# One 128x128 product per direction for the correction of both heads in a chunked delta-rule scan

## The chip, the cores and the metric

The kernel runs as one program on one core of a Trainium2 chip. The metric is the device time of one execution in microseconds. Before the change it is 1182.2 us, the median of three runs (1181.57 to 1183.22 us).

## The reference

Two layers of an encoder over 256 tokens of width 2048. Each layer normalises its input, multiplies it by one wide input matrix, feeds two groups of heads, gates both, and multiplies the result by an output matrix that is added to the residual. One group is windowed attention with a sink per head; the other is the RWKV-7 delta rule, one scan over the tokens per direction, and this is the part that the change touches:

```python
def step(S, inp):
    r_t, w_t, k_t, v_t, kk_t, a_t = inp
    s_kk = jnp.einsum('bhvk,bhk->bhv', S, kk_t)
    S = (S * w_t[:, :, None, :]
         - s_kk[..., None] * (a_t * kk_t)[:, :, None, :]
         + v_t[..., None] * k_t[:, :, None, :])
    return S, jnp.einsum('bhvk,bhk->bhv', S, r_t)
...
for d, rev in enumerate((False, True)):
    ...
    y = y + wkv_scan(rh, heads(decay), kd, vh, kk, heads(a), rev)
```

There are 16 such heads of 64 channels, two directions and 256 steps. The attention masks scores outside a band of 128 tokens on either side.

## The kernel before

**The large matrix products.** The input and output matrices are streamed from HBM as tiles of 128x1024 f32, each split on the chip into a high part (ScalarE, line 241) and the rest (VectorE, line 243). Every 128 contraction rows then cost three matmuls with 256 moving columns (lines 311 to 313): high by high, high by the rest of the activations, rest by high. The queue of these steps is called S; S.run(n) issues n of them.

**The scans** work on pairs of heads, eight pairs p per layer: head 0 of a pair lies in partitions 0 to 63, head 1 in 64 to 127. The 256 tokens are cut into NC = 4 chunks of 64. For each chunk and direction the delta rule becomes a triangular system. scan_p prepares keys, decays and values of a pair. scan_i builds the triangular matrices and inverts all 16 of a pair by doubling levels in f16, with a last refinement; its result, an inverse of 64x64 per head, direction and chunk, is copied out of PSUM into VF (line 966). scan_b then goes through the chunks i = 0 to 3, both directions side by side (direction 1 takes the chunks in reverse), and each chunk has three segments:

- a: right-hand sides (matmuls, line 993), copied to RH (ScalarE, line 995), and the outputs of the chunk before (line 978);
- b: the part of the output that comes from the state (line 1005); the **correction**, the inverse times RH, one 64x64 product per direction and head (line 1011); a product with the identity that carries the state along (line 1014); and two copies of the result into SUV (ScalarE, line 1016), which overwrite the state that lines 1005 and 1014 read;
- c: the new state (matmuls, line 1021, and VectorE, line 1023).

All operands of the correction are f32. Head 0 uses rows and columns 0 to 63 of the array, head 1 rows and columns 64 to 127.

**The order of the work.** TensorE's order is the order of the program text; the order on the other engines is made by a planner from modelled times and priorities, apart from the calls through PA and PV, which keep their order. A layer is a row of windows w. A window has 11 slots; in each slot every generator that is due issues its next segment, in the order of the list in scans(), and then S issues its share of the 64 steps, 17 or 18 matmuls. I call the matmuls of the segments of one slot a burst. A pair p runs scan_p in windows p and p+1, scan_i in p+2 and in slots 0 to 4 of p+3, and scan_b from slot 5 of window p+3 on. The correction of chunk 0 falls in slot 6 and that of chunk 1 in slot 9 of window p+3, those of chunks 2 and 3 in slots 1 and 4 of window p+4. In slots 6 and 9 scan_b of that pair comes after scan_i of the next one; in slots 1 and 4 it comes first.

**What else meets there.** In slot 8 scan_p issues a sum over heads into a PSUM tile pk, which VectorE reads with a reciprocal (kd). In slot 9 scan_p issues another such sum, pbn (both line 706), and scan_i takes a PSUM tile pd (line 937). pk, pbn, pd and scan_i's other tiles (pq and pn among them) come from one pool of two buffers, and pd gets the buffer of pk. In slot 7 the matmuls of line 937 read QF and tt, which ScalarE copies out of the pq of slot 6 (lines 931 and 899).

**The band.** A mask of 128x512 comes from HBM in one piece of 128x960 f32 with other constants (line 353), is cast to bf16 once (line 371), and is used by all attention scores of both layers (line 1092). Attention starts in slot 3 of window 10 of a layer.

Of the kernel before, what the change touches and what calls it, by code (L numbers as in the profile page):

```python
# [9 lines left out]
F32 = mybir.dt.float32  # L10
F32R = mybir.dt.float32r
F16 = mybir.dt.float16
BF16 = mybir.dt.bfloat16
U8 = mybir.dt.uint8
I32 = mybir.dt.int32
AF = mybir.ActivationFunctionType
# [5 lines left out]
T = 256  # L22
# [3 lines left out]
NP = 8  # L26
# [4 lines left out]
NC = T // CHUNK  # L31
# [13 lines left out]

STAGE_P = (([8], [4, 5, 7, 8, 10]), ([9], [0, 1, 3, 4, 5, 6, 7, 8, 9]))
STAGE_I = (list(range(SLOTS)), [0, 1, 2, 3, 4])
STAGE_B = (list(range(5, SLOTS)), [i for i in range(SLOTS) if i != 7], [7])
ATT = [
    [3, 9],  # L50
    [1, 3, 5, 6, 8, 10],
# [82 lines left out]
def hybrid_trunk_kernel(ctx, tc, xT, wi, wv, wo, par, fing, dup, iup, sink, pos, cst, out):  # L134
# [24 lines left out]
    def st(tag, shape, dt=F32, bufs=1):  # L159
        return sp.tile([128, *shape], dt, tag=tag, name=tag, bufs=bufs)  # L160
# [45 lines left out]
    class Norm:  # L206


        def add(self, sums):

            self.ps = wpair("pr")
            pr = self.ps[:, :, 0:1]
            self.rt = rt = st("rt", [2])
            self.dg = st("dg", [2, 128])
            for i, a in enumerate(sums):
                for b in range(2):
                    PE.matmul(pr[:, b], a[:, b * 128 : (b + 1) * 128], ones[:, 0:1], start=(i == 0), stop=(i == len(sums) - 1))
            with tc.high_priority(offset=100):
                V.tensor_scalar(rt, pr[:, :, 0], 1.0 / D, NORM_EPS, op0=ALU.mult, op1=ALU.add)
                G.tensor_tensor(rt, rt, mhalf[:, 0:2], op=ALU.pow)  # L220
                for b in range(2):
                    V.tensor_scalar(self.dg[:, b, :], ident, rt[:, b : b + 1], None, op0=ALU.mult)
# [113 lines left out]
    LV = cp.tile([128, NL, 2, 128], U8, name="LV")  # L336
    AB0, AB1, AL, QF = (cp.tile([128, 2, NC, 64], F16, name=n) for n in ("AB0", "AB1", "AL", "QF"))
    MSK = cp.tile([128, NC, 64], F16, name="MSK")
    EYE, NEYE, EYE2 = (cp.tile([128, 64], F16, name=n) for n in ("EYE", "NEYE", "EYE2"))
    band = cp.tile([128, 512], BF16, name="band")  # L340
    BONES = cp.tile([128, 128], F32R, name="BONES")
    FG = cp.tile([128, NKT], F32, name="FG")
    SK = cp.tile([128, DEPTH * 16], F32, name="SK")
# [3 lines left out]
    def setup():  # L347
        posi = st("t1", [T], I32, bufs=3)
        SY.dma_start(out=posi, in_=pos.to_broadcast([128, T]))
        SY.dma_start(out=FG, in_=fing)  # L350
        SY.dma_start(out=SK, in_=sink.to_broadcast([128, DEPTH * 16]))
        cin = st("mv", [C_N - C_KEEP], bufs=3)
        SY.dma_start(out=cin, in_=cst[:, C_KEEP:C_N])
        for l in range(DEPTH):
            s = DP[:, l, 0:NSH]
            V.tensor_tensor(s, PR[:, l, P_MU0 : P_MU0 + NSH], PR[:, l, P_MU1 : P_MU1 + NSH], op=ALU.add)
            V.tensor_scalar(s, s, -1.0, 1.0, op0=ALU.mult, op1=ALU.add)
            h = DP[:, l, NSH : NSH + 8]
            V.tensor_scalar(h, PR[:, l, P_KA : P_KA + 8], 0.5, None, op0=ALU.mult)
            V.tensor_scalar(DP[:, l, NSH + 8 : NSH + 16], h, -1.0, 1.0, op0=ALU.mult, op1=ALU.add)  # L360
            V.tensor_scalar(DP[:, l, NSH + 16 : NSH + 32], PR[:, l, P_A0 : P_A0 + 16], 0.5, None, op0=ALU.mult)
        V.tensor_scalar(SK, SK, 8.0, None, op0=ALU.mult)
        yield

        V.tensor_copy(
            LV.rearrange("p l s (n x) -> p (l s) n x", x=32),
            cin[:, 512 : 512 + 64 * NL].rearrange("p (n x) -> p n x", x=32).unsqueeze(2).to_broadcast([128, 2 * NL, NC, 32]),
        )
        V.memset(MSK, 1.0)
        V.memset(MSK[:, :, 0:1], 0.0)  # L370
        V.tensor_copy(band, cin[:, 0:512])
        A.activation(BONES, ones, AF.Copy, scale=0.0)
        for r in half:
            A.activation(BONES[r, r], ones[r, r], AF.Copy)
        V.tensor_copy(EYE, cin[:, 512 + 64 * NL : 576 + 64 * NL])
        V.tensor_scalar(NEYE, EYE, -1.0, None, op0=ALU.mult)
        V.tensor_scalar(EYE2, EYE, 2.0, None, op0=ALU.mult)
        yield

        AN = st("VA", [2, T])  # L380
        ang, nn = AN[:, 0], AN[:, 1]
        V.tensor_copy(ang, posi)
        yield
        PV.tensor_scalar(ang, ang, C[:, C_OFF["inv"] : C_OFF["inv"] + 1], None, op0=ALU.mult)
        yield

        def reduce_by(dst, src, period, bits, shift):
            PV.tensor_scalar(nn, src, 1.0 / period, shift, op0=ALU.mult, op1=ALU.add)
            yield
            PV.tensor_scalar(nn, nn, MAGIC, MAGIC, op0=ALU.add, op1=ALU.subtract)  # L390
            yield
            cur = src
            for p in split_const(period, bits, 4):
                PV.scalar_tensor_tensor(dst, nn, -p, cur, op0=ALU.mult, op1=ALU.add)
                cur = dst
                yield

        two_pi = 2.0 * np.pi
        yield from reduce_by(ang, ang, two_pi * 4096.0, 7, 0.0)
        for dst, shift, add in ((SIN, 0.0, 0.0), (COS, 0.25, np.pi / 2)):  # L400
            yield from reduce_by(dst, ang, two_pi, 11, shift)
            if add:
                PV.tensor_scalar(dst, dst, float(add), None, op0=ALU.add)
            PV.tensor_scalar(dst, dst, PI_IN, -PI_IN, op0=ALU.min, op1=ALU.max)
            yield
        for dst in (SIN, COS):
            PA.activation(dst, dst, AF.Sin)
        yield
        PV.tensor_scalar(SIN, SIN, C[:, C_OFF["sgn"] : C_OFF["sgn"] + 1], None, op0=ALU.mult)
        yield  # L410
# [263 lines left out]
    def layer(l):  # L674
# [141 lines left out]
        def scan_i(p, t):  # L816
# [145 lines left out]
                    )  # L962
            for d, c, h in dch:
                PE.matmul(pn[half[h], d, cs(c)], hx(FN, d, c, h), hx(TT, d, c, h), start=False, stop=True, skip_group_check=True)
            VF = st("vf", [2, NC * 64])
            A.activation(VF, pn[:, :, 0:T], AF.Copy)
            t["VF"] = VF
            yield

        def scan_b(p, t):  # L970
# [12 lines left out]
            for i in range(NC):  # L983
# [15 lines left out]
                if i > 0:  # L999
                    outputs(i - 1)  # L1000
                yield
                if i > 0:
                    for d in range(2):
                        for h in range(2):
                            PE.matmul(  # L1005
                                py[half[h], ci[d], :], MV[half[h], d, ci[d], 1, :], SUV[half[h], d, ci[d], h, :],
                                start=False, stop=False, skip_group_check=True,
                            )
                for d in range(2):
                    for h in range(2):  # L1010
                        PE.matmul(pc[half[h], 1, d, :], t["VF"][half[h], d, cs(ci[d])], RH[half[h], d, :], start=True, stop=True)  # L1011
                if 0 < i < NC - 1:
                    for h in range(2):
                        PE.matmul(pS[half[h]], ident[half[h], half[h]], here(h), start=True, stop=False, skip_group_check=True)  # L1014
# [40 lines left out]
        def scans(w):  # L1055

            gens = []
            prep = [(1, STAGE_P[1]), (0, STAGE_P[0])]
            stages = [(lag, scan_p, at[0]) for lag, at in prep]
            stages += [(4, scan_b, STAGE_B[1]), (3, scan_i, STAGE_I[1]), (2, scan_i, STAGE_I[0])]  # L1060
            stages += [(4, scan_b, STAGE_B[2]), (3, scan_b, STAGE_B[0])]
            stages += [(lag, scan_p, at[1]) for lag, at in prep]
            for lag, scan, at in stages:
                p = w - lag
                if 0 <= p < NP:
                    if (scan, p) not in chains:
                        chains[scan, p] = scan(p, L.ts[p])
                    gens.append((chains[scan, p], at))
            return gens

        def scores(j):
# [13 lines left out]
            for h in range(2):  # L1085
# [4 lines left out]
                A.activation(Sc[:, h, :, 256:257], sk.unsqueeze(1).to_broadcast([128, 2, 1]), AF.Copy)  # L1090
                for q in range(2):
                    V.tensor_tensor_reduce(
                        out=Sc[:, h, q, 0:256], in0=ps[:, q * 256 : (q + 1) * 256], in1=band[:, q * 256 : (q + 1) * 256],
                        scale=1.0, scalar=-3e38, op0=ALU.add, op1=ALU.max, accum_out=mx[:, q : q + 1],
                    )
                V.tensor_scalar(mx, mx, sk, -0.125, op0=ALU.max, op1=ALU.mult)
# [29 lines left out]

        def attend():

            scores(0)
            yield  # L1130
            flip(0)
            scores(1)
            yield
            for x in (MH, ML):
                x.more()
            for j in range(8):
                values(j)
                if j < 6:
                    scores(j + 2)
                yield  # L1140
                if j < 7:
                    flip(j + 1)
                    yield

        for w in range(NP + 2):
            window(64, *scans(w), *([(setup_, ROT.get(w, [2, 5, 9, 9]))] if l == 0 else []))
        att = attend()
        window(64, *scans(NP + 2), (att, ATT[0]))
        window(64, *scans(NP + 3), (att, ATT[1]))
        window(64, (att, ATT[2]))  # L1150
# [3 lines left out]

    queue_inputs(0)
    V.memset(QF, 0.0)

    idle = wbank("warm")
    zeros = QF.rearrange("p d c j -> p (d c j)")
# [122 lines left out]
```

## Time and profile before

| | |
|---|---|
| median of three runs | 1182.2 us |
| the profiled execution: its own time | 1180.42 us |
| its span, first to last instruction | 1178.6 us |
| mean granted TensorE clock | 0.994 of full speed |
| TensorE matmul busy | 1149.2 us (98%) |
| VectorE busy | 906.1 us (77%) |
| ScalarE busy | 777.5 us (66%) |
| GpSimd busy | 21.7 us (2%) |
| DMA queue of the loads | 164.21 MB, 42.7% of 16 engines |

PE is TensorE's matmuls, PEld its weight loads, DVE VectorE, ACT ScalarE, POOL GpSimd, SP the engine that issues the DMAs. A row of the timeline gives start, duration, engine, line, operation, the tiles written and read, and the count of instructions merged into it; in brackets stands the idle time before it and what ended it. A form such as 64*64 64x32 is the shape of the weights and of the moving operand. An f32 matmul is recorded as two passes, each with its weight load; those of lines 311 to 313 take one. Matmuls are pipelined: a row's duration contains the way through the array, so the cost of a stream is read from the distances between starts. A recorded idle time begins at the modelled end of the matmul before, so it is shorter than the delay of the start.

### The profile page before, as it was taken

The numbers are of one execution on the slowest core, as the hardware profiler recorded it, in microseconds if no ns is written. First come the engines' busy times: TensorE is split into PE (matmuls) and PEld (weight loads), VectorE is DVE, ScalarE is ACT, GpSimd is POOL, SyncE is SP. The second block draws the span as 40 slices with busy tenths as digits, with TensorE's granted clock in tenths as the row PEclk, the third lists the DMA queues.
The fourth block names the chain that finished last, engine by engine and source line by source line (L and its number), as shares of the span: only waits on it lengthen the run. The fifth ranks groups of instructions, "written<-read, shape, count | busy, mean of one in ns | idle before, by whom it ended". The sixth has DMA issues, their size and how long they took to land. (4 is left out here: it accounts for less than half of the span.)

```text
span 1178.6 us, 38072 instructions
## 1 busy us (share of the span) xinstructions
PE 1149.2 (98%) x16151; PEld 1076.2 (91%) x16151; DVE 906.1 (77%) x2017; ACT 777.5 (66%) x1955; POOL 21.7 (2%) x23
## 2 busy tenths in 40 slices
PE   8999999999999999999999999999999999999996
PEld 6998999989899999899999989999999999899996
DVE  7889978888877677766678988888887767786654
ACT  6666776786775666655556667776786666675552
POOL 0000000000000000000000000000000000000000
PEclk9999999999999999999999999999999999999998
DMA  7544433233333333477654433333333343346653
GB/s 259 167 153 131 130 107 123 96 111 102 107 102 130 130 125 122 138 239 237 212 183 169 136 130 116 115 111 116 97 112 110 119 132 126 108 140 194 212 192 119
DMA packets 60410, 166.63 MB, mean 141 GB/s; under 512 B 7728, under 2 KB 22736, under 8 KB 60240
## 3 DMA queue, kind: packets, MB, share of 16 engines
q1 hardware_dynamic: 60240, 164.21, 42.7%
q8 instruction: 126, 2.06, 0.7%
q14 instruction: 44, 0.36, 0.1%
HBM read 157.37 MB, written 4.19 MB: 137 GB/s over the span
## 5 line engine op out<-in xcount | busy, mean ns | idle before, releaser
L243 DVE TENSOR_TENSOR lo<-raw,hi 128x512 fp32r<-128x512 f32 x560 | 371.8, 687 | 114.9 <-ACT hi L241 109.7
L241 ACT ACTIVATE hi<-raw 128x512 fp32r<-128x512 f32 x560 | 330.0, 625 | 184.8 <-PE pm L312 103.6
L311 PE MATMUL pm<-XHa,hi 128*128 128x256 f32 x832 | 246.3, 296 | 2.6 <-ACT XHa L203 1.2
L311 PE MATMUL pm<-XHb,hi 128*128 128x256 f32 x832 | 243.9, 293 | 0.6 <-ACT XHb L203 0.4
L313 PE MATMUL pm<-XHb,lo 128*128 128x256 f32 x832 | 234.3, 282 | 1.7 <-DVE lo L243 1.7
L312 PE MATMUL pm<-XLb,hi 128*128 128x256 f32 x832 | 234.3, 282 | 0.4 <-DVE XLb L204 0.4
L312 PE MATMUL pm<-XLa,hi 128*128 128x256 f32 x832 | 233.8, 281 | 0.5 <-DVE XLa L204 0.3
L313 PE MATMUL pm<-XHa,lo 128*128 128x256 f32 x832 | 233.2, 280 | 0.4 <-DVE lo L243 0.4
L311 PEld LDWEIGHTS pm<-XHa,hi 128*128 128x128 f32 x832 | 156.4, 188 | 15.1 <-issue 3.2
L311 PEld LDWEIGHTS pm<-XHb,hi 128*128 128x128 f32 x832 | 157.3, 189 | 6.7 <-ACT XHb L203 0.6
L313 PEld LDWEIGHTS pm<-XHb,lo 128*128 128x128 f32 x832 | 157.4, 189 | 2.2 <-DVE lo L243 2.1
L312 PEld LDWEIGHTS pm<-XLb,hi 128*128 128x128 f32 x832 | 157.5, 189 | 0.6 <-DVE XLb L204 0.6
L312 PEld LDWEIGHTS pm<-XLa,hi 128*128 128x128 f32 x832 | 156.8, 188 | 1.0 <-DVE XLa L204 0.9
L313 PEld LDWEIGHTS pm<-XHa,lo 128*128 128x128 f32 x832 | 156.6, 188 | 0.9 <-DVE lo L243 0.9
L1016 ACT ACTIVATE suv<-pcc 64x128 f32<-64x128 f32 x128 | 34.7, 271 | 73.4 <-PE pcc L1014 49.7
L311 PE MATMUL pm<-MHa,hi 128*128 128x256 f32 x256 | 71.9, 281 | 0.0
L313 PE MATMUL pm<-MHa,lo 128*128 128x256 f32 x256 | 71.7, 280 | 0.0
L311 PE MATMUL pm<-MHb,hi 128*128 128x256 f32 x256 | 71.6, 280 | 0.0
L312 PE MATMUL pm<-MLb,hi 128*128 128x256 f32 x256 | 71.6, 280 | 0.0
L312 PE MATMUL pm<-MLa,hi 128*128 128x256 f32 x256 | 71.6, 280 | 0.0
L313 PE MATMUL pm<-MHb,lo 128*128 128x256 f32 x256 | 71.6, 280 | 0.0
L311 PEld LDWEIGHTS pm<-MHa,hi 128*128 128x128 f32 x256 | 48.1, 188 | 0.8 <-issue 0.8
(291 smaller groups left out, 2312.1 us busy)
## 6 DMA issues: line engine op xcount, KB each, us to landing
raw<-wi SPq DMA_DIRECT2D x207, 512.0 KB
raw<-wo SPq DMA_DIRECT2D x64, 512.0 KB
raw<-wv SPq DMA_DIRECT2D x8, 512.0 KB
rrot<-u SPq DMA_DIRECT2D x80, 32.0 KB
vg<-xT SPq DMA_DIRECT2D x16, 128.0 KB
xd<-vg SPq DMA_DIRECT2D x16, 128.0 KB
vg<-xd SPq DMA_DIRECT2D x16, 128.0 KB
g<-dup SPq DMA_DIRECT2D x16, 97.0 KB
```

The source lines that it names most:

```text
L241: A.activation(hi[:, q], raw[:, q], AF.Copy)
L243: V.tensor_tensor(lo[:, q], raw[:, q], hi[:, q].bitcast(F32), op=ALU.subtract)
L311: PE.matmul(pm, wh, rh[:, kk, :], start=(kk == 0), stop=False)
L312: PE.matmul(pm, wh, rl[:, kk, :], start=False, stop=False)
L313: PE.matmul(pm, wl, rh[:, kk, :], start=False, stop=(kk == 15))
L1016: A.activation(here(h), pc[half[h], 1], AF.Copy)
```

## The change

Four things are done together.

- VF becomes a tile of its own for the whole run, [128, 2, NC, 128] f32, filled with zeros by GpSimd at the start. The inverse of head 0 is written to rows 0 to 63 and columns 0 to 63 of each 128x128 block, that of head 1 to rows and columns 64 to 127: two ScalarE copies of 64 partitions in the place of one copy of 128 partitions.
- The correction is one product per direction with 128x128 weights and 64 moving columns, and it stands first in its segment, ahead of line 1005.
- In slots 6 and 9 the segment of scan_b is issued before that of scan_i (a fourth list in STAGE_B).
- The band mask leaves the load at the start (448 instead of 960 columns). Each layer loads it at the beginning of window 9 into a tile under the tag th, and casts it to bf16 under the tag sl just ahead of the first scores. The tile dg of the norm moves to the tag ysq.

```diff
-STAGE_B = (list(range(5, SLOTS)), [i for i in range(SLOTS) if i != 7], [7])
+STAGE_B = ([5, 7, 8, 10], [i for i in range(SLOTS) if i != 7], [7], [6, 9])
...
-            self.dg = st("dg", [2, 128])
+            self.dg = st("ysq", [2, 128])
...
+    VF = cp.tile([128, 2, NC, 128], F32, name="VF")
...
-    band = cp.tile([128, 512], BF16, name="band")
...
-        cin = st("mv", [C_N - C_KEEP], bufs=3)
-        SY.dma_start(out=cin, in_=cst[:, C_KEEP:C_N])
+        cin = st("mv", [C_N - C_KEEP - 512], bufs=3)
+        SY.dma_start(out=cin, in_=cst[:, C_KEEP + 512 : C_N])
...
-        V.tensor_copy(band, cin[:, 0:512])
...
-            VF = st("vf", [2, NC * 64])
-            A.activation(VF, pn[:, :, 0:T], AF.Copy)
-            t["VF"] = VF
+            for h in range(2):
+                A.activation(VF[half[h], :, :, h * 64 : (h + 1) * 64], pn[half[h], :, 0:T].rearrange("p d (c j) -> p d c j", j=64), AF.Copy)
...
+                for d in range(2):
+                    PE.matmul(pc[:, 1, d, :], VF[:, d, ci[d], :], RH[:, d, :], start=True, stop=True)
                 if i > 0:
                     for d in range(2):
                         for h in range(2):
...
-                for d in range(2):
-                    for h in range(2):
-                        PE.matmul(pc[half[h], 1, d, :], t["VF"][half[h], d, cs(ci[d])], RH[half[h], d, :], start=True, stop=True)
...
-            stages += [(4, scan_b, STAGE_B[1]), (3, scan_i, STAGE_I[1]), (2, scan_i, STAGE_I[0])]
+            stages += [(4, scan_b, STAGE_B[1]), (3, scan_b, STAGE_B[3]), (3, scan_i, STAGE_I[1]), (2, scan_i, STAGE_I[0])]
             stages += [(4, scan_b, STAGE_B[2]), (3, scan_b, STAGE_B[0])]
...
+            wide = st("th", [512])
+            SY.dma_start(out=wide, in_=cst[:, C_KEEP : C_KEEP + 512])
+            yield
+            L.band = st("sl", [512], BF16)
+            V.tensor_copy(L.band, wide)
             scores(0)
...
+        att = attend()
         for w in range(NP + 2):
+            if w == NP + 1:
+                next(att)
...
+    G.memset(VF, 0.0)
```

More of the change, by code (lines that the diff above doesn't have):

```diff
@@ L366, in setup @@
             LV.rearrange("p l s (n x) -> p (l s) n x", x=32),
-            cin[:, 512 : 512 + 64 * NL].rearrange("p (n x) -> p n x", x=32).unsqueeze(2).to_broadcast([128, 2 * NL, NC, 32]),
+            cin[:, 0 : 64 * NL].rearrange("p (n x) -> p n x", x=32).unsqueeze(2).to_broadcast([128, 2 * NL, NC, 32]),
         )
@@ L374, in setup @@
             A.activation(BONES[r, r], ones[r, r], AF.Copy)
-        V.tensor_copy(EYE, cin[:, 512 + 64 * NL : 576 + 64 * NL])
+        V.tensor_copy(EYE, cin[:, 64 * NL : 64 + 64 * NL])
         V.tensor_scalar(NEYE, EYE, -1.0, None, op0=ALU.mult)
@@ L1092, in scores @@
                     V.tensor_tensor_reduce(
-                        out=Sc[:, h, q, 0:256], in0=ps[:, q * 256 : (q + 1) * 256], in1=band[:, q * 256 : (q + 1) * 256],
+                        out=Sc[:, h, q, 0:256], in0=ps[:, q * 256 : (q + 1) * 256], in1=L.band[:, q * 256 : (q + 1) * 256],
                         scale=1.0, scalar=-3e38, op0=ALU.add, op1=ALU.max, accum_out=mx[:, q : q + 1],
@@ L1143, in attend @@
                     yield
+        att = attend()
         for w in range(NP + 2):
+            if w == NP + 1:
+                next(att)
             window(64, *scans(w), *([(setup_, ROT.get(w, [2, 5, 9, 9]))] if l == 0 else []))
-        att = attend()
         window(64, *scans(NP + 2), (att, ATT[0]))
```

## The prediction

> **What bounds the kernel now.** I read the page first, then TensorE's waits, then the timelines of slots 4 to 9 of a window in the middle of layer 1.
>
> ```profile
> span 1178.6 us, 38072 instructions
> ## 1 busy us (share of the span) xinstructions
> PE 1149.2 (98%) x16151; PEld 1076.2 (91%) x16151; DVE 906.1 (77%) x2017; ACT 777.5 (66%) x1955; POOL 21.7 (2%) x23
> ```
>
> ```profile
> PE pd L937 <- DVE kd L256: 5.8, 10, 0.7
> ```
>
> ```profile
> PE pd L937 <- ACT tt L899: 2.0, 1, 2.0
> ```
>
> TensorE is busy for 98% of the span. So each part of the change is worth what it adds to TensorE's stream or takes from the few waits in it. The largest of these (total, times, longest, in us) is the wait of pd for the reciprocal kd. ScalarE at 66% looks free; below it turns out not to be so in one place.
>
> **The product itself.** Its present cost and that of its neighbours, from TensorE's timeline:
>
> ```profile
> L1011 PE MATMUL pcc<-rh,vf 64*64 64x64 f32 x512 | 26.1, 220 | 0.0
> ```
>
> ```profile
> 799.33 0.40 PE L706 MATMUL pbn<-ip,BONES 128*128 128x256 f32 x2
> 800.27 0.30 PE L937 MATMUL pd<-QF,tt 64*64 64x32 f16 x16 [0.54 <-DVE kd L256]
> 800.40 0.44 PE L1005 MATMUL py<-suv,mv 64*64 64x64 f32 x8
> 800.66 0.41 PE L1011 MATMUL pcc<-rh,vf 64*64 64x64 f32 x8
> 800.89 0.40 PE L1014 MATMUL pcc<-suv,C 64*64 64x128 f32 x4
> 801.23 0.38 PE L311 MATMUL pm<-XHa,hi 128*128 128x256 f32 x1
> ```
>
> There are 512 records, 8 in each of 64 bursts. From the first start of L1011 to that of L1014 it is 0.23 us: the two heads run at the same time, in separate quarters of the array, so the eight make four steps of 0.058 us. Merging the heads therefore halves a count of instructions that were already running in pairs.
>
> The new form is not in the trace: four records per burst, two per direction, with 128x128 f32 weights and 64 columns. The nearest rows are the sums of the norm, with the same weights and type and one column:
>
> ```profile
> 24.59 0.28 PE L313 MATMUL pm<-XHa,lo 128*128 128x256 f32 x1
> 24.70 1.84 PE L217 MATMUL pr<-C,mv 128*128 128x1 f32 x16
> 26.41 0.37 PE L311 MATMUL pm<-XHa,hi 128*128 128x256 f32 x1
> ```
>
> ```profile
> 250.10 0.45 PE L978 MATMUL py<-suv,GE 128*64 128x64 f32 x8
> 250.48 0.31 PE L937 MATMUL pd<-QF,tt 64*64 64x32 f16 x16
> ```
>
> ```profile
> 412.18 0.28 PE L313 MATMUL pm<-XHa,lo 128*128 128x256 f32 x1
> 412.39 0.45 PE L1011 MATMUL pcc<-rh,vf 64*64 64x64 f32 x8
> 412.77 0.39 PE L311 MATMUL pm<-XHa,hi 128*128 128x256 f32 x1
> ```
>
> Sixteen of them take 26.41 - 24.70 = 1.71 us, 0.107 each, although they stream one column: the weights set the pace. The array is entered without a break (24.59 to 24.70, 0.11), while a change to quarters costs 0.21 (412.18 to 412.39). After a short f32 product the next shape comes 0.15 later: the last of L978 starts at 250.10 + 0.45 - 0.22 = 250.33, L937 at 250.48. So the new product ahead of a burst adds 0.11 to enter, three steps of 0.107 and 0.15 to leave, less the 0.21 that entering the quarters costs today: 0.37 us. The bounds of the step are 0.058 (the present one, if the loads hid) and 0.107; I take the upper one, which the same weights show.
>
> The Trainium skill says the same of the loads in "TensorE: Matmul & The Clock Gate", section "LDWEIGHTS (loading the stationary operand)", as columns over 1.2, 107 ns for 128. But its section "Back-to-back issue gap" gives about 81 ns per matmul for a sustained stream of loads and matmuls; with that the added product would be 0.29, an estimate, and it is weighed among the rivals.
>
> Burst by burst, over both layers:
> - Slots 1 and 4, 32 bursts: 0.37 - 0.23 = +0.14 each, 4.5 us.
> - Slot 6, 16 bursts. In 14 the correction is last, and it also pays for the way out, as the next rows show: L1011 starts at 789.18, L311 at 789.53, 0.35. Without it L311 would follow the last L895 (789.05 + 0.28 - 0.18 = 789.15) by the 0.11 that it follows the last L937 by (105.00 to 105.11). So it costs 0.27 now, and +0.10 with the change: 1.4 us. The other two bursts hold nothing else (412.39); they go from 0.59 (412.18 to 412.77) to 0.11 + 0.32 + 0.11 = 0.54: -0.1 us.
> - Slot 9, 16 bursts: +0.14, less some 0.03 because L937 now comes last, with its shorter way out: 1.8 us.
>
> ```profile
> 788.90 0.30 PE L928 MATMUL pq<-tv,AB 64*64 64x32 f16 x16
> 789.05 0.28 PE L895 MATMUL pq<-EYE,tv 64*64 64x32 f16 x16
> 789.18 0.42 PE L1011 MATMUL pcc<-rh,vf 64*64 64x64 f32 x8
> 789.53 0.39 PE L311 MATMUL pm<-XHa,hi 128*128 128x256 f32 x1
> ```
>
> ```profile
> 104.88 0.30 PE L937 MATMUL pd<-QF,tt 64*64 64x32 f16 x16 [0.73 <-DVE kd L256]
> 105.11 0.39 PE L311 MATMUL pm<-XHa,hi 128*128 128x256 f32 x1
> ```
>
> ```profile
> 682.48 0.30 PE L937 MATMUL pd<-QF,tt 64*64 64x32 f16 x16 [0.54 <-DVE kd L256]
> ```
>
> Together TensorE gets **7.6 us** more work.
>
> **The wait that the order in slot 9 fills.** In the rows at 799.33, L937 stands still until the reciprocal has freed pd's buffer, and everything of scan_b queues behind it. VectorE's row:
>
> ```profile
> 798.46 1.76 DVE L256 RECIPROCAL kd<-pk 128x256 f32<-128x256 f32 x1
> ```
>
> It ends at 800.22, 0.89 after the burst began. With scan_b first, L937 comes after two L706 (0.23), the correction (0.32 + 0.15), L1005 (0.23) and L1014 (0.11 + 0.11): 1.16 us after the burst began, so the wait is covered, with 0.27 us to spare. It also stands in two bursts without scan_b (104.88 and 682.48, 0.73 and 0.54), which stay. That leaves 5.8 - 1.27 = 4.5 us in eight bursts. The true delay is 0.07 larger each: L937 follows the second L706 (799.33 + 0.12) by 0.82, against 0.21 undisturbed, 0.61 and not 0.54. So **5.1 us** go.
>
> **The second copy of VF.** It is in slot 4, and the next reader is in slot 6, so VF itself is not late. But ScalarE works through without a pause up to slot 7:
>
> ```profile
> 784.08 0.60 ACT L966 ACTIVATE vf<-pn 128x512 f32<-128x512 f32 x1
> 784.57 0.38 ACT L931 ACTIVATE QF<-pq 128x256 f16<-128x256 f32 x1
> ```
>
> ```profile
> 788.07 0.30 ACT L995 ACTIVATE rh<-pcc 128x128 f32<-128x128 f32 x1
> ```
>
> ```profile
> 789.37 0.51 ACT L454 ACTIVATE vg<-u,DP 128x256 f32<-128x256 f32 x1
> 789.97 0.63 ACT L256 ACTIVATE FR<-FR 64x512 f32<-64x512 f32 x1
> ```
>
> ```profile
> 791.47 0.38 ACT L899 ACTIVATE tt<-pq 128x256 f16<-128x256 f32 x1
> ```
>
> ```profile
> 791.66 0.28 PE L313 MATMUL pm<-XHa,lo 128*128 128x256 f32 x1
> 791.90 0.31 PE L937 MATMUL pd<-QF,tt 64*64 64x32 f16 x16
> ```
>
> ```profile
>   ACT tt L899: 5.8, 11
> ```
>
> tt ends at 791.85 and L937 starts at 791.90, 0.24 after the matmul before it where 0.21 is usual: TensorE already waits for ScalarE here, by a hair. The last row, from the view of L937, counts 11 such ends of an idle time, weight loads included; eight are windows with scan_b. A copy with 64 partitions streams the same 512 elements, so I price the second at the 0.50 us between the starts at 784.08 and 784.57. The idle 0.09 at 789.88 takes a part, and TensorE is itself 0.11 later from slot 6: 0.50 - 0.09 - 0.11 = 0.30 us in eight bursts, **2.4 us**. Bounds: nothing, if the planner orders QF and tt before other copies, and 0.50 x 10 windows = 5.0. RH, too, is later by 0.50; today it ends at 788.37, 0.53 before the burst in which the correction now comes first. That leaves nearly nothing, and I take no wait.
>
> **The band.** Three edges, all small; VectorE's rows of the start, with the cast at 26.66:
>
> ```profile
> 25.09 0.96 DVE L365 CAST LV<-mv 128x1536 uint8<-128x1536 f32 x1 [0.87 <-DMA mv<-cst]
> ```
>
> ```profile
> 26.66 0.42 DVE L371 CAST band<-mv 128x512 bf16<-128x512 f32 x1
> 27.67 0.48 DVE L222 TENSOR_SCALAR dg<-C,rt 128x128 f32<-128x128 f32 x2 [0.59 <-POOL rt L220]
> ```
>
> VectorE waited 0.87 us for the piece that now loses 512 of 960 columns. What follows on it is held by dg, which waits for the norm and not for a load. I take 0.3 us of gain, between 0 and 0.87. The two later loads enter SP's queue, ahead of weights, at the start of window 9, when scan_p, the last user of the tag th, is done. I take nothing, because weights are split ahead of their use; the bound is half of that 0.87 per layer, another 0.9. Each layer's cast is 0.42 us of VectorE under the matmuls of window 10; without that cover one more would cost 0.4. The tags dg and ysq are in use at no common time. GpSimd writes its zeros before the first matmuls need anything of it, on an engine with 21.7 us of work; uncovered, 1024 columns would cost a few times the 0.42 of 512 above, some 1 to 2 us, at the start alone.
>
> **Sum.** +7.6 - 5.1 + 2.4 - 0.3 = **+4.6 us**. The profiled execution takes 1180.4 (span 1178.6 and 1.8 around it), so it would take 1185.0. The median of the runs lies 1.8 above that execution, so I forecast **1186.8 us**, slower by 0.4%. About 0.2%, 2.4 us, is what a measurement of this kernel tells from no change.
>
> **The rivals.**
>
> 1. *The load hides and the product steps at the pace of its columns* (step 0.058). The added product is then 0.22 us, 0.15 less than above, and 64 x 0.15 = 9.6: TensorE's term falls from 7.6 to -2.0 and the sum to -5.0: **1177.2**, faster. Its place is every correction, and it decides the sign of the sum from a step of 0.083 downward (64 bursts x 3 steps x 0.024 = 4.6). Against it speaks L217 with one column. By the Trainium skill's 81 ns in the section named above the sum would be -0.4, an estimate. Chance 0.13.
> 2. *ScalarE's order turns out better.* The moved segments change the modelled times; if QF and tt come ahead of other copies, the 2.4 us vanish and so may the 2.0 us wait for tt in the waits above: 4.6 - 2.4 - 2.0 = +0.2, **1182.4**. For it: ScalarE does have pauses elsewhere. Against: nothing in the diff names those copies. Chance 0.16.
> 3. *The wait at pd stays*, because the reciprocal moves later by as much as L937 does. 4.6 + 5.1 = 9.7: **1191.9**. Against: its only input, pk, is ready at slot 8, one slot ahead. Chance 0.11.
> 4. *The correction, now first, waits for RH* in the eight full windows, and slot 6 queues behind it. With 0.03 us of slack left, 0.3 us of disorder in ScalarE costs 8 x 0.3 = 2.4: **1189.2**. Chance 0.12.
>
> **How the numbers follow.** The forecast has 0.48, with its own range from 1183.5 to 1190.0 (ScalarE's term from 0 to 5, the start and the band from -0.6 to +0.9). Slower by over 0.2%: most of the forecast (0.41) and rivals 3 and 4, 0.64. Within 0.2%: the rest of the forecast, most of rival 2, the middle of rival 1, 0.20. Faster: most of rival 1 and the better side of rival 2, 0.16. The range goes from 1179 to 1193.
>
> **What would show it.** Right: the new L1011 with 256 records about 0.107 us apart, 0.37 per burst over the burst without it; the wait of pd for kd down to two of 1.3 us; L937 in slot 7 some 0.3 us behind its predecessor beyond the usual 0.21. Wrong: L1011's records 0.06 to 0.08 apart, pd still idle in windows with scan_b, slot 7 without delay, or slot 6 starting late behind RH.

## The result and the profile after

The changed kernel takes 1190.1 us, the median of 4 runs (1189.1 to 1193.2), beside 1182.0 for the kernel before on the same chip: a ratio of 1.0071, 95% interval 1.0051 to 1.0092. That is 8.2 us slower. The profiled execution took 1189.8 us. One execution of the kernel with the band alone took 2884.9 us where its other eleven took 1180.4 to 1183.1, and is left out of its figures. The page after:

```profile
span 1188.0 us, 37577 instructions
## 1 busy us (share of the span) xinstructions
PE 1159.7 (98%) x15895; PEld 1092.2 (92%) x15895; DVE 906.5 (76%) x2018; ACT 787.2 (66%) x1971; POOL 22.9 (2%) x24
```

The span grew by 9.4 us (from 1178.6). TensorE has 256 instructions fewer and is busy 10.5 us longer. Its waits (total, times, longest, in us):

```profile
PE pd L936 <- ACT tt L898: 5.6, 8, 2.5
...
PE pd L936 <- DVE kd L256: 1.3, 2, 0.7
...
PE pza L690 <- DVE bv L256: 1.1, 5, 0.2
PE pm L311 <- ACT VA L588: 1.0, 2, 0.5
```

The wait of pd for kd fell from 5.8 us to two of 1.3 in all. The wait of pd for tt went from 2.0 us, once, to 5.6 in eight windows. A wait of pza for bv, 0.5 us twice before, now comes five times. The wait for VA, which ScalarE copies for the attention once per layer, went from 0.4 us in all to 1.0.

The same slots as those quoted of before, in TensorE's timeline after: first slots 6 and 7 of one window, then slot 9.

```profile
836.34 0.28 PE L313 MATMUL pm<-XHa,lo 128*128 128x256 f32 x1
836.46 0.55 PE L1001 MATMUL pcc<-rh,VF 128*128 128x64 f32 x4
836.94 0.30 PE L927 MATMUL pq<-tv,AB 64*64 64x32 f16 x16
...
839.40 0.28 PE L313 MATMUL pm<-XHa,lo 128*128 128x256 f32 x1
840.13 0.30 PE L936 MATMUL pd<-QF,tt 64*64 64x32 f16 x16 [0.45 <-ACT tt L898]
840.34 0.68 PE L1038 MATMUL py<-C,ysq 64*64 64x64 f32 x16
...
847.57 0.40 PE L705 MATMUL pbn<-ip,BONES 128*128 128x256 f32 x2
847.80 0.55 PE L1001 MATMUL pcc<-rh,VF 128*128 128x64 f32 x4
848.28 0.45 PE L1005 MATMUL py<-suv,mv 64*64 64x64 f32 x8
...
848.99 0.39 PE L311 MATMUL pm<-XHa,hi 128*128 128x256 f32 x1
```

From the product to the next shape it is 0.48 us in both places (836.46 to 836.94, 847.80 to 848.28). In the trace the four records start 0.055, 0.11 and 0.11 us after one another (0.277 in all), and the next shape 0.205 after the last. Slot 9 is now 1.42 long (847.57 to 848.99), where it was 1.90 (799.33 to 801.23), and its rows hold no wait.

In slot 7, L936 starts 0.73 after the last L313 (839.40 to 840.13), where it was 0.24 before. But the row behind it, line 1038 (1041 before), has an operand that is late as well: ysq, which VectorE writes. VectorE's rows from slot 5 to slot 7, and TensorE's row that reads ysq, before:

```profile
786.60 0.69 DVE L243 TENSOR_TENSOR lo<-raw,hi 128x512 fp32r<-128x512 f32 x1 [1.51 <-ACT hi L241]
...
791.59 0.41 DVE L256 TENSOR_TENSOR ysq<-py,yv 128x256 f32<-128x256 f32 x1
```

```profile
792.05 0.68 PE L1041 MATMUL py<-C,ysq 64*64 64x64 f32 x16
```

And VectorE's after:

```profile
834.99 0.69 DVE L243 TENSOR_TENSOR lo<-raw,hi 128x512 fp32r<-128x512 f32 x1 [2.43 <-ACT hi L241]
...
839.87 0.41 DVE L256 TENSOR_TENSOR ysq<-py,yv 128x256 f32<-128x256 f32 x1
```

Both times the row that reads ysq starts 0.05 to 0.06 us behind ysq's end (792.00 and 792.05, 840.28 and 840.34). Counted from the last L313, ysq is ready at 0.34 before (792.00 - 791.66) and at 0.88 after: 0.54 later, which is what the burst grew by. It is so in seven of the eight windows. VectorE is late because it waits longer for hi, which ScalarE makes behind the copies of VF, and from there to ysq it has no pause. Only in the window with the longest wait for tt is ysq ready long before tt. The list of waits has 5.6 us for tt and only 0.5 for ysq, because line 936 stands first and its wait hides that of the next row.

I added up the length of every burst, from the last large matmul before it to the first behind it, by kind of burst; before and after differ so:

| where | us |
|---|---|
| product, slots 1 and 4 (32 bursts, 0.16 each) | +5.1 |
| product, slot 6 (14 bursts, 0.126 each; two lone ones -0.2) | +1.5 |
| product, slot 9 (16 bursts, 0.147 each) | +2.4 |
| slot 9, the wait for kd in eight bursts | -5.1 |
| slot 7 in eight bursts (ysq in seven, tt in one) | +5.1 |
| slot 10, the wait for bv | +1.4 |
| the wait for VA, once per layer | +0.6 |
| slot 8 -0.4, large matmuls -1.0, attention +0.2, start -0.4 | -1.6 |
| sum | +9.4 |

### The profile page after: what moved, and what is told of

The parts are those of the page before. It is cut to its first block, busy times and chain, and to the rows that moved or that the text cites. A ratio compares the mean times of both kernels' runs of the same rounds, so it can differ in the third digit from the quotient of the medians.

```text
span 1188.0 us, 37577 instructions
## 1 busy us (share of the span) xinstructions
PE 1159.7 (98%) x15895; PEld 1092.2 (92%) x15895; DVE 906.5 (76%) x2018; ACT 787.2 (66%) x1971; POOL 22.9 (2%) x24
## 5 line engine op out<-in xcount | busy, mean ns | idle before, releaser
L313 PE MATMUL pm<-XHb,lo 128*128 128x256 f32 x832 | 233.5, 281 | 1.2 <-DVE lo L243 1.2
L313 PE MATMUL pm<-XHa,lo 128*128 128x256 f32 x832 | 234.0, 281 | 0.4 <-DVE lo L243 0.4
L313 PEld LDWEIGHTS pm<-XHb,lo 128*128 128x128 f32 x832 | 156.9, 189 | 1.4 <-DVE lo L243 1.4
L313 PEld LDWEIGHTS pm<-XHa,lo 128*128 128x128 f32 x832 | 157.3, 189 | 0.9 <-DVE lo L243 0.9
L313 PE MATMUL pm<-MHa,lo 128*128 128x256 f32 x256 | 71.8, 281 | 0.0
L313 PE MATMUL pm<-MHb,lo 128*128 128x256 f32 x256 | 71.7, 280 | 0.0
```

The lines of the kernel that those rows point to most:

```text
L313: PE.matmul(pm, wl, rh[:, kk, :], start=False, stop=(kk == 15))
```

## The experiments

Four theories were put to the test: that the order of segments pays by the wait in slot 9; that the product costs TensorE time and would cost more in another place; that slot 7 is late because of the second copy of VF; and that the band is free. Ratios are to the kernel before, run on the same chip; 0.001 of it is 1.2 us.

**The order alone**, in the kernel before:

```diff
-STAGE_B = (list(range(5, SLOTS)), [i for i in range(SLOTS) if i != 7], [7])
+STAGE_B = ([5, 7, 8, 10], [i for i in range(SLOTS) if i != 7], [7], [6, 9])
...
-            stages += [(4, scan_b, STAGE_B[1]), (3, scan_i, STAGE_I[1]), (2, scan_i, STAGE_I[0])]
+            stages += [(4, scan_b, STAGE_B[1]), (3, scan_b, STAGE_B[3]), (3, scan_i, STAGE_I[1]), (2, scan_i, STAGE_I[0])]
```

> The kernel before with one part of the change alone: in slots 6 and 9 the segment of scan_b is issued ahead of that of scan_i. Product, copy of VF and band stay as before. Theory A (the order fills the wait of pd for kd, whatever the product): the eight waits of 0.6 go, -5.3 us; about 1.4 of it comes back in slot 10, where pza waits for bv; sum -4 us. Rival B (the wait went only because TensorE came later with the longer product): a part of the waits of pd for kd stays, and the time stays within 1 us of before.

Measured: 1177.8 us, ratio 0.9963 [0.9949, 0.9976], so 4 us faster. Slot 9 lost 4.9 us, slot 10 gained 2.1. The waits:

```profile
PE pza L691 <- DVE bv L256: 2.1, 9, 0.2
PE pd L937 <- ACT tt L899: 1.8, 1, 1.8
...
PE pd L937 <- DVE kd L256: 1.2, 2, 0.7
```

The order is the part of the change that pays, and two fifths of what it takes from slot 9 come back one slot later: TensorE is early there and waits for VectorE. Slot 7 shows only the one wait that was there before.

**The order in slot 9 only**, slot 6 as before ([5, 6, 7, 8, 10] and [9] in the lists above):

> The kernel before with the new order in slot 9 alone; slot 6 keeps scan_i first. Theory A (all of the gain of the new order comes from the wait of pd for kd in slot 9): the same as with both slots moved, -3 to -4 us. Rival B (slot 6 has a share, because the copies into SUV can start earlier): 1 us or more behind the kernel with both slots moved.

Measured: 1178.6, ratio 0.9974 [0.9965, 0.9983]; slot 9 -5.1, slot 10 +1.8. Most of the gain is slot 9's. The intervals of the two orders overlap, so what slot 6 adds, if anything, isn't told apart.

**The product and everything else, in the old order** (the diff above undone in the changed kernel):

> The changed kernel with the old order of the segments in slots 6 and 9 (block-diagonal VF, one 128x128 product per direction first in its segment, band per layer). Theory A (product and copy are the loss, the order is the gain): slots 1 and 4 +0.16 each as in the changed kernel, slot 9 +0.3 because the product now stands between two 64x64 groups, the waits of pd for kd back at 10, slot 7 +0.5 in eight windows: some +13 to +16 us over before. Rival B (the order is what costs, by upsetting the other engines): less than the changed kernel's +8.

Measured: 1202.6, ratio 1.0166 [1.0148, 1.0184], some 20 us slower than before and more than I expected. Its waits:

```profile
PE pd L936 <- DVE kd L256: 7.4, 11, 0.8
PE pd L936 <- ACT tt L898: 4.3, 8, 2.3
```

Slot 9 is 7.5 us longer than before in its 12 bursts with L705. The wait for kd accounts for 1.6. The rest, 5.9 or 0.49 per burst, is the product in a worse place: behind line 936 it stands between two shapes in quarters, so the array changes shape once more in and out. That is its 0.15 of the table above and another 0.34, which the next experiment measures by itself. My expectation had 0.3 a burst for it and no growth of the wait for kd. With the product, the order is worth 10 us (span 1198.0 against 1188.0), not 5.

**The product second in its segment**, in the changed kernel:

```diff
-                for d in range(2):
-                    PE.matmul(pc[:, 1, d, :], VF[:, d, ci[d], :], RH[:, d, :], start=True, stop=True)
                 if i > 0:
...
+                for d in range(2):
+                    PE.matmul(pc[:, 1, d, :], VF[:, d, ci[d], :], RH[:, d, :], start=True, stop=True)
```

> The changed kernel with the 128x128 product behind line 1005 in its segment, not first. Theory A (each change between the whole array and quarters costs a drain, and the first place saves it): in slots 1, 4 and 9 the burst enters quarters for L1005, leaves them for the product and enters them again; 0.2 to 0.3 us more per burst in 48 bursts, +9 to +14 us over the changed kernel. Rival B (the place in the segment does not matter, since the loads hide the drain): the same time as the changed kernel.

Measured: 1204.9, ratio 1.0199 [1.0185, 1.0213], 15 us more in the span than the changed kernel. Slot 9 in its timeline:

```profile
858.49 0.39 PE L705 MATMUL pbn<-ip,BONES 128*128 128x256 f32 x2
858.82 0.45 PE L1003 MATMUL py<-suv,mv 64*64 64x64 f32 x8
859.19 0.66 PE L1008 MATMUL pcc<-rh,VF 128*128 128x64 f32 x4
859.78 0.33 PE L1011 MATMUL pcc<-suv,C 64*64 64x128 f32 x2
...
860.26 0.39 PE L311 MATMUL pm<-XHa,hi 128*128 128x256 f32 x1
```

The burst lasts 1.77 us (858.49 to 860.26), 0.35 more than with the product first, with the same matmuls. Over all the bursts of slots 1, 4 and 9 it is 0.31 to 0.34 each. So the place ahead of the 64x64 groups saves about 0.33 us per burst, twice what the product adds there (0.15 to 0.16). The Trainium skill states in "TensorEngine Tiling (Array Packing)", section "Key Properties", that a change of the tiling mode drains TensorE; these rows put the price at about 0.33 us for a way in and out.

**The copy in two halves alone**, in the kernel before, and **two copies of the same number of elements cut the other way**, by direction, 128 partitions each:

```diff
-            A.activation(VF, pn[:, :, 0:T], AF.Copy)
+            for h in range(2):
+                A.activation(VF[half[h]], pn[half[h], :, 0:T], AF.Copy)
```

```diff
-            A.activation(VF, pn[:, :, 0:T], AF.Copy)
+            for d in range(2):
+                A.activation(VF[:, d], pn[:, d, 0:T], AF.Copy)
```

> The kernel before, with VF copied out of PSUM in two halves of 64 partitions; nothing else is changed. Theory A (the second copy delays ScalarE up to tt, and TensorE waits for it in slot 7): the start of L937 in slot 7 is 0.73 after the matmul before it and not 0.24, in eight windows; +4 to +5 us. Rival B (the second copy is hidden, and the delay in slot 7 comes from another order of ScalarE's work in the changed kernel): within 1 us of before.

> The kernel before, with VF copied in two instructions of 128 partitions by 256 elements (one per direction) in the place of one of 512. Theory A (what costs is the length: each copy of 64 partitions streams all 512 elements again): only the fixed part of one more instruction is added, about 0.1 us, slot 7 +0.1 in eight windows, +1 us at most. Rival B (what costs is one more instruction in ScalarE's queue and another order of the planner): as with the two half copies, +9 us.

Measured: 1190.9, ratio 1.0072 [1.0057, 1.0086], for the halves, and 1180.7, ratio 1.0001 [0.9992, 1.0010], for the directions. ScalarE's timelines, the halves first:

```profile
791.61 1.20 ACT L967 ACTIVATE vf<-pn 64x512 f32<-64x512 f32 x2
792.84 0.39 ACT L931 ACTIVATE QF<-pq 128x256 f16<-128x256 f32 x1
```

```profile
784.99 0.66 ACT L967 ACTIVATE vf<-pn 128x256 f32<-128x256 f32 x2
785.54 0.39 ACT L931 ACTIVATE QF<-pq 128x256 f16<-128x256 f32 x1
```

The halves hold ScalarE for 1.23 us until QF starts, the directions for 0.55, the single copy for 0.49 (784.08 to 784.57 in the prediction). So it is not a second instruction as such that costs but how the copy is cut: each half streams 512 elements per partition, as the whole does. And the whole lets QF start 0.11 before its own end (784.08 + 0.60); here the first half doesn't overlap with the second, nor the second with QF. The waits of the kernel with halves:

```profile
PE pd L937 <- DVE kd L256: 7.4, 11, 0.8
PE pd L937 <- ACT tt L899: 5.7, 8, 2.5
```

This part alone, without the product and the order, makes the kernel as slow as the whole change, 9 us and not the 4 to 5 expected: slot 7 +6.4, slot 9 +1.9, the waits for VA +0.7, and +0.6 in the rest of this execution. ysq is 0.67 later in seven of the eight windows. In the old order the wait for kd grows too, from 5.8 to 7.4. Why VectorE's reciprocal then comes later against TensorE was not followed up.

**One copy in the changed kernel**, as the other side of the same question:

```diff
-            for h in range(2):
-                A.activation(VF[half[h], :, :, h * 64 : (h + 1) * 64], pn[half[h], :, 0:T].rearrange("p d (c j) -> p d c j", j=64), AF.Copy)
+            A.activation(VF[:, :, :, 0:64], pn[:, :, 0:T].rearrange("p d (c j) -> p d c j", j=64), AF.Copy)
```

> The changed kernel with one ScalarE copy of 128 partitions and 512 columns into the left half of every block of VF, in the place of the two copies of 64 partitions. It leaves out the block-diagonal placement: head 1's inverse lands in head 0's columns, so its part of the correction is not the reference's; shapes, matmuls and order are those of the changed kernel. Theory (the two half copies cost 1.2 us of ScalarE where one costs 0.5, and that makes tt late in slot 7): the delay of L936 in slot 7 falls from 0.73 to about 0.25 us, and the time is 4 to 6 us below the changed kernel, that is +9.0 for the product, -5.4 for the wait in slot 9 and +1.4 in slot 10 against the kernel before: 1.002 to 1.004 of it. Rival (slot 7 is late because the order or the product shifts TensorE's place against ScalarE, not because of the copy): slot 7 keeps its delay and the time stays at 1.007.

Measured: 1182.5, ratio 1.0015 [1.0006, 1.0024]. The copy holds ScalarE for 0.49 us until QF starts. The waits:

```profile
PE pd L936 <- ACT tt L898: 1.7, 1, 1.7
...
PE pd L936 <- DVE kd L256: 1.3, 2, 0.7
```

Slot 7 is 5.9 us shorter than in the changed kernel and the span 6.1; the wait for VA is back at 0.4 us. About 0.9 of the 5.9 lies in one window and is only moved: the large matmuls behind it are as much longer. So the product and the order together cost 1.8 us more than the kernel before, and the second copy costs the rest, about 6.6 us by the ratios (0.0056 x 1181). The rest of the program is that of the changed kernel, so this shows that the copy makes slot 7 late. Both of its late operands come back: tt, and ysq, which is ready 0.22 to 0.25 us behind the last L313 in layer 2 and not 0.88.

**Ways to keep the halves and lose the wait.** First head 1's half copied by VectorE (the call on A becomes V.tensor_copy where h is 1), then QF and tt put ahead of ScalarE's other ready work:

```diff
-                A.activation(t_sub(QF), flat4(pq[:, :, 0:128]), AF.Copy)
-                if turned:
-                    turned()
+                with tc.high_priority(offset=PRIO_TC):
+                    A.activation(t_sub(QF), flat4(pq[:, :, 0:128]), AF.Copy)
+                    if turned:
+                        turned()
```

> The changed kernel, with the copy of head 1's half of the inverse made by VectorE and that of head 0 by ScalarE. Theory A (of the changed kernel's +8, about 5 are the second copy on ScalarE; the product costs 9 and the order gives back 5): slot 7 back to a start of L937 within 0.3 of the matmul before it, 4 to 5 us less than the changed kernel, so +3 to +4 over before. Rival B (the copy is a delay wherever it is made, because VectorE is just as full there): the wait of slot 7 goes and another for VectorE of like size comes; the time stays at that of the changed kernel.

> The changed kernel with ScalarE's copies to QF and tt (L930, L898) given priority over its other ready work. Theory 1 (slot 7 is late only through ScalarE's order; in the order's place the work has room elsewhere): the delay of L936 in slot 7 falls from 0.73 to about 0.25, and the time is 3 to 5 us below the changed kernel, 1.003 of the kernel before. Theory 2 (ScalarE has no slack between slot 4 and slot 7, so what is overtaken is late next): slot 7's delay is smaller, but a wait for RH, for FR or for the splits of the weights takes its place, and the time stays within 1 us of the changed kernel, 1.007.

Measured: 1191.0, ratio 1.0084 [1.0071, 1.0098], and 1191.3, ratio 1.0096 [1.0079, 1.0113]: neither better than the changed kernel. Some of TensorE's waits, with VectorE's copy first:

```profile
PE pd L936 <- ACT tt L898: 4.6, 5, 1.9
...
PE pcc L1005 <- ACT rh L997: 0.6, 1, 0.6
```

And with tt first:

```profile
PE py L1039 <- DVE ysq L256: 4.3, 8, 0.8
```

With VectorE's copy slot 7 is 3.5 us shorter in the eight full windows, but the planner makes another order and waits for tt and RH come up in windows at the edges of a layer, +3.9 us in slots 7 and 9 there. With tt first, tt is in time (L937 0.24 behind the last L313), and eight waits for ysq of line 1039, the next row of slot 7, stand in its place. In seven of the eight windows slot 7 is as long as in the changed kernel (2.35 us against 2.32 in layer 2), with ysq ready at 0.91 us where it was 0.88. So it is ysq and not tt that sets slot 7 there. In the eighth window slot 7 is 2.7 us shorter, but other waits follow (for suv and hi, 0.95 and 1.20 us), and the granted clock is 0.50 from 308 to 316 us: this one window is 3.6 us longer than in the changed kernel, of 4.2 in the span. ysq put first on VectorE was not tried.

**The band alone**, in the kernel before (load, cast and tags as in the change; the norm's tile stays):

```diff
-        cin = st("mv", [C_N - C_KEEP], bufs=3)
+        cin = st("mv", [C_N - C_KEEP - 512], bufs=3)
...
+            wide = st("th", [512])
+            SY.dma_start(out=wide, in_=cst[:, C_KEEP : C_KEEP + 512])
+            yield
+            L.band = st("sl", [512], BF16)
+            V.tensor_copy(L.band, wide)
```

> The kernel before, with the band loaded and cast once per layer and the load at the start shortened; nothing else is changed. Theory A (both ends are hidden but for the wait at the start): -0.5 to 0 us. Rival B (the load of 256 KB ahead of the weights in SP's queue, or its wait for the tag th, makes a weight tile late at the start of window 9): +1 to +2 us, with a wait of TensorE for hi or lo near 355 or 930 us.

Measured: 1182.0, ratio 1.0002 [0.9992, 1.0011]. No cost and no gain can be told.

**The order, with bv first on VectorE.** The order alone left 2.1 us at bv. So:

```diff
-            PV.tensor_tensor(bv, pb[:, 0:T], VV, op=ALU.mult)
+            with tc.high_priority(offset=PRIO_TC):
+                PV.tensor_tensor(bv, pb[:, 0:T], VV, op=ALU.mult)
```

> The kernel before with the new order of segments in slots 6 and 9, and on VectorE the product bv of scan_p is given priority over the other work that is ready. Theory: the order alone takes some 5 us from slot 9 but leaves 2.1 us of it in slot 10, where TensorE (L690, pza) now waits for bv; with bv first the wait in slot 10 falls from 2.1 us to under 1, and the time is 1 to 2 us below the order alone (0.995 of the kernel before). Rival: VectorE has no slack there, so the operation that bv overtakes becomes late in its turn, or bv was held by its operands and not by VectorE's order; then the time is that of the order alone (0.9963) or above.

> The kernel before with the priority for bv on VectorE alone; the order of segments stays as before. Theory: bv sets TensorE's start in slot 10 only once slot 9 is free of its wait; before, the wait for bv is 0.5 us in two places and slot 10 is no shorter with bv first. So the time is within 1 us of the kernel before (0.999 to 1.001), and the gain of bv first behind the new order (slot 10 -2.1 us) belongs to the pair. Rival: bv first is a better order of VectorE by itself; then this kernel is 2 us or more below the kernel before (0.998 or less). Other side: bv overtakes what slot 9 needs, kd, and the wait there grows: above 1.001.

Measured: 1173.7, ratio 0.9942 [0.9929, 0.9954], with the order; 1180.4, ratio 0.9991 [0.9982, 1.0000], without it. TensorE at the start of slot 10, with the order alone and with bv first:

```profile
761.04 0.45 PE L1021 MATMUL pcc<-suv,bt 128*64 128x64 f32 x8
761.70 0.39 PE L691 MATMUL pza<-TW,duh 97*128 97x256 f32 x1 [0.21 <-DVE bv L256]
```

```profile
760.29 0.45 PE L1022 MATMUL pcc<-suv,bt 128*64 128x64 f32 x8
760.67 0.39 PE L691 MATMUL pza<-TW,duh 97*128 97x256 f32 x1
```

L691 follows by 0.38 instead of 0.66. Slot 10 is 2.1 us shorter over the windows that the order had made late and 0.6 in two that waited before as well; the span is 2.0 shorter. By itself bv first gives some 2 us at most, perhaps nothing: before, TensorE came to slot 10 too late to wait, but for two times. Together they make the fastest kernel of this study, 0.6% below the kernel before and 1.3% below the changed one.

## Why the prediction was right, and where its sizes were off

The forecast was slower by 4.6 us; measured are 8.2, and 9.4 between the two profiled executions. The sign is right and the three causes are those named: product, order and second copy. But two sizes of the product were off and cancelled, and the second copy was priced too low and followed to one operand of three. Point by point:

- **The product: +7.6, measured +9.0.** The mechanism is the one named: the weights set the pace, for the weight loads of the four records start 0.109 to 0.116 us apart, and the array must be left again. That 0.48 comes out against 0.47 is partly luck: three steps take 0.277 us and not 3 x 0.107 = 0.32, because the first is 0.055, and leaving costs 0.205 and not 0.15. With 0.117 to enter, a burst gains 0.117 + 0.48 - 0.21 = 0.39, as it does on the average over the bursts, and not 0.37; the small excess counts 62 times. Rival 1 is out: three steps of 0.058 would be 0.17. The rate of 81 ns from the Trainium skill's "TensorE: Matmul & The Clock Gate", section "Back-to-back issue gap", which that page gives for 128 moving columns, would make three steps 0.24 and not 0.277, an estimate; each of the two steps behind the first is longer than it, 0.11. The load time of the section "LDWEIGHTS (loading the stationary operand)", 107 ns for 128 columns, fits these f32 rows.
- **The wait in slot 9: -5.1, measured -5.1.** kd is down to two waits of 1.3, as forecast, and rival 3 is out. What the prediction lacks is what comes next on the path: with slot 9 short, slot 10 waits for bv, +1.4. The order alone gives back 2.1, and bv first gets it back, which shows it.
- **The second copy: +2.4, measured +5.7** (slot 7 +5.1, the wait for VA +0.6). Its price was mis-sized: "I price the second at the 0.50 us between the starts". The 0.50 holds an overlap of 0.10 with the next instruction, and with the cut in halves two such overlaps are lost. ScalarE's rows after:

```profile
831.73 1.20 ACT L965 ACTIVATE VF<-pn 64x512 f32<-64x512 f32 x2
832.95 0.38 ACT L930 ACTIVATE QF<-pq 128x256 f16<-128x256 f32 x1
```

  1.22 less 0.49 is 0.73 added, not 0.50. TensorE's own lateness and ScalarE's pauses take 0.25 together (0.20 in the prediction), so tt is 0.48 later against TensorE, and so is L936. Of slot 7's operands the prediction follows tt alone, and there its path is wrong in seven of the eight windows: ysq decides, 0.54 later over hi and VectorE, and seven times that is 3.8. It did so before the change as well (line 1041 at 792.05, ysq's end at 792.00), which the prediction didn't look at. In the eighth window tt decides: 0.5 us, and 0.8 of lower clock, told below. VA is a third operand that the copy makes late: the wait is 0.8 to 1.3 us in every kernel where ScalarE copies both halves, and 0.4 in every other one. The upper bound given, 5.0, was the better guess.
- **Start and band: -0.3, measured -0.4 at the start,** reached 71 us into the run. It can't be put down to the band: with the band alone the same place comes 0.4 us later than in the kernel before, and in four kernels that start like the kernel before it comes 0.3 to 0.7 later. The band alone has no effect on the time that can be measured.
- **Rival 2** (ScalarE's order turns out better) didn't happen. When QF and tt were put first by hand, its 2.4 us didn't vanish either, since ysq stayed late. **Rival 4** (the correction waits for RH) isn't among the waits after. It came up once, with VectorE's copy.

## What to carry to other kernels

Joining two products that already run side by side in parts of the array saves instructions and no time: compare the distance between starts of the joined form, weights' width included, with that of the pair. Price an added instruction by the elements that it streams per partition, and take into account whether the next one starts before its end. A list of waits names the operand that TensorE stood for first; look whether the operand of the next row is as late, as ysq was behind tt. When a wait on the path is removed, look up which operand is the next to be late and give its maker priority in the same edit: here the order alone was worth 4 us, and with bv first 7.

## What the hardware showed that was not expected

The two halves of VF hold ScalarE for 1.22 us, 0.61 each, and the whole copy for 0.49, though each of the three lasts 0.60. The Trainium skill's "ScalarE: Activation LUTs", section "What ACT_TABLE_LOAD costs", gives an overlap of about 93 ns between instructions that follow one another. The whole copies and the copies by direction agree with it. So does head 0's half where QF follows it, as in the kernel with VectorE's copy:

```profile
830.79 0.59 ACT L969 ACTIVATE VF<-pn 64x512 f32<-64x512 f32 x1
831.28 0.37 ACT L930 ACTIVATE QF<-pq 128x256 f16<-128x256 f32 x1
```

It holds the engine for 0.49 us. Head 1's half, in partitions 64 to 127, overlaps neither with what stands ahead of it nor with what follows: 0.01 to 0.03 us lie between them after, and with tt first, where QF stands between the halves. So it isn't the count of 64 partitions that costs the overlap. Why head 1's half loses it is not shown.

A stretch of lower clock can follow a wait. In the window with the longest wait for tt, TensorE's rows after are these; the last two are of a stretch of several large matmuls at the same distance:

```profile
301.60 0.30 PE L936 MATMUL pd<-QF,tt 64*64 64x32 f16 x16 [2.47 <-ACT tt L898]
301.75 0.96 PE L1038 MATMUL py<-C,ysq 64*64 64x64 f32 x16
...
304.49 0.41 PE L313 MATMUL pm<-XHb,lo 128*128 128x256 f32 x1
304.70 0.41 PE L311 MATMUL pm<-XHb,hi 128*128 128x256 f32 x1
```

Large matmuls follow by 0.21 us instead of 0.117, and line 1038 takes 0.96 instead of 0.68. The stretch from 285 to 320 us by its busy times, clock (the column after POOL) and DMA: after, with one copy, and with the product in the old order:

```profile
285.00:320.00 35.00, 32.53 (x586) 30.47 (x586) 27.64 (x61) 28.39 (x74) 1.31 (x1) 0.95 0.34 107
```

```profile
285.00:320.00 35.00, 33.32 (x530) 31.40 (x524) 29.13 (x64) 26.17 (x70) 1.31 (x1) 0.95 0.33 101
```

```profile
285.00:320.00 35.00, 32.71 (x593) 30.36 (x592) 29.57 (x65) 29.40 (x75) 1.32 (x1) 1.00 0.34 107
```

The waits for tt in this window are 2.5, 1.7 and 2.3 us. So the length of the wait doesn't decide alone whether the clock falls. Of the fourteen profiled executions of this study eleven have such a stretch here, and three have none: those of the order alone, of the band alone and of the last row, behind waits of 1.8, 2.0 and 2.3 us. What decides is open. The kernel before has one too (0.95), on large matmuls. After, it falls on the burst of slot 7, which grew by 1.29 us where the others grew by 0.54. So the 0.8 of lower clock above is moved from one row of the table to another and isn't a cost of the change: the large matmuls behind that burst take 0.8 less.
